# Where the compressed-value product and two spare transposes stand between the matmuls of a hybrid attention layer

## The chip, the cores and the metric

The kernel runs on one core of one Trainium2 chip. The metric is the device time of one execution in microseconds; the median of three runs of the kernel before is 369.53 us (369.27 to 370.02). A difference of about 0.2% (0.74 us) or less is not told apart from none.

## The reference

One decoder layer over 256 tokens of width 1024, in float32. What matters here:

```python
h = rmsnorm(x, norm1_g[layer])
proj = h @ w_in[layer]           # NSA q, 6 k/v parts, gates | MoBA q, k, v | 2 merge gates
...
y_nsa = nsa_attention(to_q(q), to_q(q_r), kc, vc, to_kv(k_s), to_kv(v_s),
                      to_kv(k_w), to_kv(v_w), gates)
...
y_moba = moba_attention(to_kv(qm), to_kv(km), to_kv(vm))
...
mixed = g_nsa * (y_nsa @ w_up_nsa[layer]) + g_moba * (y_moba @ w_up_moba[layer])
x = x + mixed @ w_out[layer]
h2 = rmsnorm(x, norm2_g[layer])
u = jax.nn.relu(h2 @ w_ff1[layer])
x = x + (u * u) @ w_ff2[layer]
```

Native sparse attention (NSA) adds three products per head: `gc[0] * o_cmp + gc[1] * o_sel + gc[2] * o_win`, over 15 compressed keys, the selected blocks and a window. With 256 tokens the selected blocks and the window are both all earlier tokens. MoBA is causal attention of 8 further heads.

## The kernel before, in words

Weights come in chunks of 1 MB (`CHUNKS`), one DMA each, three buffers deep. To multiply in float32, each chunk is split into a high part (`whi`, cast on ScalarE, L114) and a low part (`wlo`, difference on VectorE, L116) of type fp32r, and each product is three fp32r matmuls, a "triple" (`mm3`: high x high, high x low, low x high). All matmuls are recorded under one line, L243.

A chunk is a *slot*. `run_slot` issues the slot's matmuls in order and, at given fractions of it, the events that were registered with `at(position, function)`. The order on each engine is therefore written out by these positions; it doesn't depend on any planner. Chunks 0 to 11 are the projections (`xstat`: activations are the stationary operand, weights stream past, outputs 512 wide for q, qm, km and vm); chunk 11 (`C_VM + 1`) is the second half of vm. From chunk 12 on, the merge gates (gm, 12 to 19), then upn (20, 21), upm (22, 23), wout (24 to 27) and ff1 have the weights as stationary operand and stream 256 activations past (`wstat`). So chunk 11 ends with 128x512 matmuls, and chunk 12 begins with 128x256 ones. From chunk 31 on, ff2 and ff1 chunks alternate.

Attention runs in six *units* d = 0 to 5, threaded through the slots 9 to 21: units 0 to 3 are NSA (kind "n": one pair of heads p, the selected and the window branch, b = 1 and 2), units 4 and 5 are MoBA (kind "m": two pairs of heads). For unit d, slot 9 + 2d issues the scores (`d_scores`), the maxima on VectorE and the exponentials on ScalarE; slot 10 + 2d issues `d_norm` (VectorE, writes P at L580) and `d_trans`, near its end: twelve 128x128 transposes of P into the score banks Sa and Sb (L596), copied to PT by ScalarE (L598) and VectorE (L600). In the next slot, behind the next unit's scores, `d_pv` multiplies PT by the values: eight fp32 matmuls with 64 output rows each, two of them side by side in the array (128\*64). Here this is called the *P-V break*: the streams of full-array fp32r matmuls stop, and a few instructions of other shapes and types stand between. `d_yevac` then reads the sum y in bank yb (ScalarE L628, VectorE L629). Each fp32 matmul shows as two passes in the trace.

In an NSA unit, y has a further summand, the *compressed product*: one fp32 matmul of the block-diagonal compressed values (`bdv`) with the transposed compressed probabilities (`pcT`). In the kernel before it is the last thing that `d_trans` issues, and it opens the sum (start flag).

Behind unit 5's P-V break, in slot 21, the rest of upn, then upm, wout and the first ff1 chunk and a half are one unbroken run of 128x256 fp32r matmuls, until `x1_rows` transposes x in the middle of slot 29 (L883).

A helper from the ff2 stage, used in `seven_mms` for the last triple ahead of an ff1 chunk, issues a 512-wide triple as two 256-wide ones:

```python
def mm3_halves(o, lh, ll, rh, rl, first, last):
    r = mm3(o, lh, ll, rh, rl, first, last)[:int(first)]
    return r + [m for x in (slice(0, 256), slice(256, 512))
                for m in mm3(o[:, x], lh, ll, rh[:, x], rl[:, x], first, last)[int(first):]]
```

Of the kernel before, what the change touches and what calls it, by code (L numbers as in the profile page):

```python
# [36 lines left out]
C_KVB, C_Q, C_QM, C_KM, C_VM, C_GM, C_UPN, C_UPM, C_WOUT, C_FF = (  # L37
    2, 4, 6, 8, 10, 12, 20, 22, 24, 28)
# [7 lines left out]
def hybrid_layer(ctx: ExitStack, tc: tile.TileContext, gxd, w, w1c, small, const, gf, out):  # L46
    nc = tc.nc
    act, dve, pool, pe = nc.scalar, nc.vector, nc.gpsimd, nc.tensor
# [14 lines left out]
    def bank(tag, name):  # L63
        return ps.tile([128, 512], F32, name=name, tag=tag)
# [8 lines left out]
    def acc_tile():  # L73
        return next_bank("acc")
# [6 lines left out]
    def s_tile(x):  # L81
        if "s" not in pools:
            early_stack.close()
            pools["s"] = at_stack.enter_context(tc.tile_pool(name="ps_s", bufs=1, space=PS))
        return pools["s"].tile([128, 2, 512], F32, name="S" + "ab"[x])
# [35 lines left out]
    ident = cp.tile([128, 128], F32, name="ident")  # L121
# [120 lines left out]
    def mm(o, l, r, start, stop):  # L242
        pe.matmul(o, l, r, start=start, stop=stop, skip_group_check=True)  # L243

    def mm3(o, lh, ll, rh, rl, first, last):
        return [lambda: mm(o, lh, rh, first, False),
                lambda: mm(o, lh, rl, False, False),
                lambda: mm(o, ll, rh, False, last)]
# [7 lines left out]
    def xstat(c, n, accs, kts):  # L256

        r = []
        h, l = hi[c], lo[c]
        order = [(t, k) for t in range(2) for k in range(4)]  # L260
        if c < 2:
            order.sort(key=lambda e: e[1])
        for t, k in order:
            kt = kts[k]
            if True:
                lh, ll = (a[:, kt, t * 128:(t + 1) * 128] for a in (hTh, hTl))
                r += mm3(accs[t][:, :n], lh, ll, h[:, k * n:(k + 1) * n],
                         l[:, k * n:(k + 1) * n], kt == 0, kt == 7)
        return r

    def wstat(o, c, off, nk, ncol, ah, al, ks=None, first=0, last=None):
# [123 lines left out]
    bdv = ap_.tile([128, 4, 128], F32, name="bdv")  # L395
    pcT = ap_.tile([128, 256], F32, name="pcT")
# [5 lines left out]
    U = {}  # L402
# [120 lines left out]
    def s_views(d, t):  # L523
        S = U[d]["S"][1 - t]
        n = 128 + 128 * t
        return S[:, :, 0:2 * n].rearrange("p j (x k) -> p j x k", x=2)
# [56 lines left out]
    def d_trans(d):  # L583

        S, P = U[d]["S"], U[d]["P"]
        kind, p, _ = PAIRS[d][0]
        PT = ap_.tile([128, 4, 384], F32, name="PT")
        U[d]["PT"] = PT
        v = PT.rearrange("p (x j) k -> p j x k", x=2)
        for t, cs in ((1, (128, 256)), (0, (0,))):  # L590
            T = s_views(d, t)
            for j in range(2):
                for x in range(2):
                    for c in cs:
                        o = c % 256 if t == 0 else c - 128
                        pe.transpose(T[:, j, x, o:o + 128], P[:, 2 * x + j, c:c + 128], ident)  # L596
            if t:
                act.activation(v[:, :, :, 128:384], T, AF.Copy)  # L598
            else:
                dve.tensor_copy(v[:, :, :, 0:128], T)  # L600
        if d == 0:
            U["y"] = bank("yb", "yb").rearrange("p (a q) -> p a q", a=2)
        if kind == "n":
            mm(U["y"][:, p % 2], bdv[:, p, :], pcT, True, False)

    def d_pv(d):
        PT = U[d]["PT"]
        for x, (kind, p, b) in enumerate(PAIRS[d]):
            y = U["y"][:, p % 2]

            ts = (1, 0) if kind == "n" else (0, 1)
            for t in ts:
                n0 = 128 * t
                for j in range(2):
                    if kind == "n":
                        v = kvb[:, t, b * 128 + j * 64:b * 128 + (j + 1) * 64]
                    else:
                        v = vm[:, t, (2 * p + j) * 64:(2 * p + j + 1) * 64]
                    rhs = PT[:, 2 * x + j, 0:256] if t == 0 else PT[:, 2 * x + j, 256:384]
                    mm(y[j * 64:(j + 1) * 64, n0:256], v, rhs, kind == "m" and t == 0,  # L620
                       t == ts[1] and (kind == "m" or b == 2))

    def d_yevac(d):
        kind, p, _ = PAIRS[d][0]
# [6 lines left out]
    def unit_events(s):  # L631
        d = (s - 9) // 2
        if not 9 <= s <= 21:
            return
        if s % 2 == 0:
            at(0.1, d_norm, d)
            at(0.97 if s == 12 else 0.78, d_trans, d)
            return
        if d < 6:
            at(0.1, d_scores, d)  # L640
        if d > 0:
            at(0.1, d_pv, d - 1)
        if d < 6:
            at(0.11, d_max, d)
            at(0.2 if s > 12 else 0.5, d_exp, d, 1)
            at(0.22 if s > 12 else 0.52, d_exp, d, 0)
        if d > 0:
            at(0.12, d_yevac, d - 1)
# [4 lines left out]
    for sec, c0, n in groups:  # L653
        if sec in ("q", "qm", "km"):
            tm[sec] = ap_.tile([128, 2, 512], F32, name="qtm", bufs=2)
        if sec in ("kvb", "q"):
            accs = [ps_e.tile([128, 512], F32, name=f"{sec}acc{t}") for t in range(2)]
        else:
            accs = [acc_tile(), acc_tile()]
        for i in range(2):  # L660
            c = c0 + i
# [84 lines left out]
            elif i == 1:  # L746
                at(0.49 if sec == "vm" else 0.5, evac_tm, sec, 0, accs[0], n)
                if sec != "vm":
                    at(1.0, evac_tm, sec, 1, accs[1], n)
            run_slot(xstat(c, n, accs, range(4 * i, 4 * i + 4)))  # L750


# [30 lines left out]
    for g in range(8):  # L783
        c = C_GM + g
# [31 lines left out]
    for sec, c0, kind, evac in (("upn", C_UPN, "n", upn_evac), ("upm", C_UPM, "m", upm_evac)):  # L816
        for i in range(2):
            c = c0 + i
# [13 lines left out]
            accs = [acc_tile(), acc_tile()]  # L832
# [54 lines left out]
    for i in range(4):  # L887
        c = C_WOUT + i
# [144 lines left out]
    order = PARTS[0] + PARTS[1]  # L1033
# [226 lines left out]
```

## Time and profile before

| | |
|---|---|
| median of 3 runs | 369.53 us |
| profiled execution, its own time | 370.05 us |
| its span, first to last instruction | 368.2 us |
| TensorE busy, granted clock | 98%, 0.996 |
| VectorE, ScalarE busy | 87%, 66% |
| DMA | 66.34 MB, 180 GB/s |

In the rows quoted below, a timeline row has start, duration, engine, line, operation, output<-inputs, array rows\*columns, shape and count; neighbours of one name are merged into one row. Matmuls are pipelined: their durations overlap, and what counts is the distance between starts. A window row has the stretch, its width, and for each engine its busy time and the count of instructions, then the granted clock, the DMA share and GB/s. "Idle before" in brackets names what ended the engine's wait.

### The profile page before, as it was taken

The numbers are of one execution on the slowest core, as the hardware profiler recorded it, in microseconds if no ns is written. First come the engines' busy times: TensorE is split into PE (matmuls) and PEld (weight loads), VectorE is DVE, ScalarE is ACT, GpSimd is POOL, SyncE is SP. The second block draws the span as 40 slices with busy tenths as digits, with TensorE's granted clock in tenths as the row PEclk, the third lists the DMA queues.
The fourth block names the chain that finished last, engine by engine and source line by source line (L and its number), as shares of the span: only waits on it lengthen the run. The fifth ranks groups of instructions, "written<-read, shape, count | busy, mean of one in ns | idle before, by whom it ended". The sixth has DMA issues, their size and how long they took to land.

```text
span 368.2 us, 6524 instructions
## 1 busy us (share of the span) xinstructions
PE 360.7 (98%) x2658; PEld 331.8 (90%) x2658; DVE 320.6 (87%) x466; ACT 241.3 (66%) x367; POOL 3.4 (1%) x14
## 2 busy tenths in 40 slices
PE   8999999999999999999999999999999999999993
PEld 7997787879989999999999999999999999999983
DVE  4988979998967769767878999999999999999984
ACT  5984765777746657526455887867666777676623
POOL 1010000000000000000000000000000000000000
PEclk9999999999999999999999999999999999999998
DMA  7978326333433333533583666455556666554003
GB/s 275 407 306 309 128 105 228 114 116 122 182 136 134 115 117 129 215 116 114 189 326 121 227 228 216 171 180 178 188 212 230 228 230 226 195 189 180 12 3 114
DMA packets 11262, 66.34 MB, mean 180 GB/s; under 512 B 1248, under 2 KB 2784, under 8 KB 3936
## 3 DMA queue, kind: packets, MB, share of 16 engines
q1 hardware_dynamic: 10368, 64.35, 47.5%
q10 hardware_dynamic: 864, 1.57, 1.2%
q8 instruction: 21, 0.34, 0.4%
q14 instruction: 9, 0.07, 0.1%
HBM read 64.87 MB, written 1.05 MB: 179 GB/s over the span
## 4 chain that ended last, share of the span: by engine, by line
PE 96%; issue 1%; DVE 0%; POOL 0%; ACT 0%; POOLq 0%; DVEq 0%
PE acc L243 64%; PE o L243 10%; PE yb L243 5%; PE tp L243 4%; PE qacc L243 3%; PE kvbacc L243 3%; PE Sa L243 2%; PE Sa L596 1%; PE tp L338 1%; PE yb L156 1%; PE Sb L596 1%; PE Sb L243 1%; PE o L883 0%; PE tp L409 0%; DVE x L1137 0%
## 5 line engine op out<-in xcount | busy, mean ns | idle before, releaser
L116 DVE TENSOR_TENSOR wlo<-raw,whi 128x1024 fp32r<-128x1024 f32 (+3 forms) x83 | 105.0, 1286 | 4.4 <-ACT whi L114 4.3
L114 ACT ACTIVATE whi<-raw 128x1024 fp32r<-128x1024 f32 (+3 forms) x82 | 89.9, 1118 | 25.9 <-PE acc L243 16.2
L243 PE MATMUL acc<-h2h,whi 128*128 128x256 f32 x256 | 71.0, 277 | 0.0
L243 PE MATMUL acc<-h2l,whi 128*128 128x256 f32 x256 | 70.9, 277 | 0.0
L243 PE MATMUL acc<-h2h,wlo 128*128 128x256 f32 x256 | 70.8, 277 | 0.0
L243 PEld LDWEIGHTS acc<-h2l,whi 128*128 128x128 f32 x256 | 48.2, 188 | 0.0
L243 PEld LDWEIGHTS acc<-h2h,whi 128*128 128x128 f32 x256 | 48.1, 188 | 0.0
L243 PEld LDWEIGHTS acc<-h2h,wlo 128*128 128x128 f32 x256 | 48.1, 188 | 0.0
L986 ACT ACTIVATE whi<-wt 128x2048 fp32r<-128x2048 f32 x14 | 26.9, 1922 | 29.0 <-PE acc L243 28.1
L243 PE MATMUL acc<-hTh,wlo 128*128 128x256 f32 x128 | 36.8, 287 | 0.0
L243 PE MATMUL acc<-hTl,whi 128*128 128x256 f32 x128 | 35.7, 279 | 0.0
L243 PE MATMUL acc<-hTh,whi 128*128 128x256 f32 x128 | 35.7, 279 | 0.0
L988 DVE TENSOR_TENSOR wlo<-wt,whi 128x2048 fp32r<-128x2048 f32 x14 | 32.0, 2284 | 0.1
L243 PEld LDWEIGHTS acc<-hTh,wlo 128*128 128x128 f32 x128 | 24.3, 190 | 1.4 <-issue 1.3
L243 PE MATMUL acc<-whi,hTh 128*128 128x512 f32 (+1 forms) x64 | 25.3, 395 | 0.0
L243 PE MATMUL acc<-wlo,hTh 128*128 128x512 f32 (+1 forms) x64 | 25.0, 391 | 0.0
L243 PE MATMUL acc<-whi,hTl 128*128 128x512 f32 (+1 forms) x64 | 24.6, 385 | 0.0
L979 DVE TENSOR_TENSOR sl<-raw,sh 128x1536 fp32r<-128x1536 f32 x14 | 24.5, 1750 | 0.0
L243 PEld LDWEIGHTS acc<-hTh,whi 128*128 128x128 f32 x128 | 24.0, 188 | 0.1
L243 PEld LDWEIGHTS acc<-hTl,whi 128*128 128x128 f32 x128 | 24.0, 188 | 0.0
L977 ACT ACTIVATE sh<-raw 128x1536 fp32r<-128x1536 f32 x14 | 20.8, 1488 | 3.3 <-PE acc L243 3.3
L243 PE MATMUL acc<-mxh,whi 128*128 128x256 f32 x64 | 18.0, 281 | 0.0
(308 smaller groups left out, 868.4 us busy)
## 6 DMA issues: line engine op xcount, KB each, us to landing
raw<-in_ff_dram SPq DMA_DIRECT2D x32, 1024.0 KB, 4.9
raw<-in_gm_dram SPq DMA_DIRECT2D x8, 1024.0 KB, 4.8
raw<-in_wout_dram SPq DMA_DIRECT2D x4, 1024.0 KB, 4.8
raw<-in_q_dram SPq DMA_DIRECT2D x2, 1024.0 KB, 5.0
raw<-in_qm_dram SPq DMA_DIRECT2D x2, 1024.0 KB, 6.3
raw<-in_km_dram SPq DMA_DIRECT2D x2, 1024.0 KB, 6.2
raw<-in_vm_dram SPq DMA_DIRECT2D x2, 1024.0 KB, 4.8
raw<-in_upn_dram SPq DMA_DIRECT2D x2, 1024.0 KB, 5.9
```

The source lines that it names most:

```text
L114: act.activation(hi[c][:, a:b], raw[c][:, a:b], AF.Copy)
L116: dve.tensor_tensor(lo[c][:, a:b], raw[c][:, a:b], hi[c][:, a:b].bitcast(F32), op=ALU.subtract)
L156: pe.transpose(warm[:, 0:128], ident, ident)
L243: pe.matmul(o, l, r, start=start, stop=stop, skip_group_check=True)
L338: pe.transpose(tp[:, j * 256 + t * 128:j * 256 + t * 128 + 128], src[:, t, (2 * i + j) * 128:(2 * i + j + 1) * 128], ident)
L596: pe.transpose(T[:, j, x, o:o + 128], P[:, 2 * x + j, c:c + 128], ident)
L977: act.activation(singles[c][0], v, AF.Copy)
L979: dve.tensor_tensor(singles[c][1], v, singles[c][0].bitcast(F32), op=ALU.subtract)
L986: act.activation(hi[c], v, AF.Copy)
L988: dve.tensor_tensor(lo[c], v, hi[c].bitcast(F32), op=ALU.subtract)
```

## The change

Three edits, all on TensorE's instructions; the other engines' instructions and their order stay the same.

1. In units 0 to 3 the compressed product is issued at the end of `d_pv` instead of the end of `d_trans`. It now closes the sum, and the first P-V matmul opens it. For this the wide half (256 columns) comes ahead of the narrow half (128 columns) in NSA units, as it already did in MoBA units.
2. Behind unit 5's P-V matmuls two transposes of the identity are issued into the free score bank; nothing reads them.
3. The last triple of chunk 11 goes through `mm3_halves`: six 256-wide matmuls instead of three 512-wide ones.

```diff
@@ xstat @@
-                r += mm3(accs[t][:, :n], lh, ll, h[:, k * n:(k + 1) * n],
-                         l[:, k * n:(k + 1) * n], kt == 0, kt == 7)
+                f = mm3_halves if c == C_VM + 1 and (t, k) == order[-1] else mm3
+                r += f(accs[t][:, :n], lh, ll, h[:, k * n:(k + 1) * n],
+                       l[:, k * n:(k + 1) * n], kt == 0, kt == 7)
@@ d_trans @@
         if d == 0:
             U["y"] = bank("yb", "yb").rearrange("p (a q) -> p a q", a=2)
-        if kind == "n":
-            mm(U["y"][:, p % 2], bdv[:, p, :], pcT, True, False)
@@ d_pv @@
-            ts = (1, 0) if kind == "n" else (0, 1)
-            for t in ts:
-                n0 = 128 * t
+            for t, n0 in ((0, 0), (1, 128)):
                 for j in range(2):
...
-                    mm(y[j * 64:(j + 1) * 64, n0:256], v, rhs, kind == "m" and t == 0,
-                       t == ts[1] and (kind == "m" or b == 2))
+                    mm(y[j * 64:(j + 1) * 64, n0:256], v, rhs,
+                       t == 0 and (kind == "m" or b == 1), t == 1 and kind == "m")
+        if kind == "n":
+            mm(y, bdv[:, p, :], pcT, False, True)
+        elif d == 5:
+
+            pace = s_tile(0)
+            for x in range(2):
+                pe.transpose(pace[:, 0, x * 128:(x + 1) * 128], ident, ident)
```

Unit 1 on TensorE, behind its transposes (slot 12 ends, slot 13 begins with unit 2's scores). Before:

```order
L596 MATMUL Sa<-ident,P 128x128 x8
L596 MATMUL Sb<-ident,P 128x128 x4
L243 MATMUL yb<-pcT,bdv 128x256
L243 MATMUL acc<-hTh,wlo 128x256
L243 MATMUL acc<-hTh,whi 128x256
L243 MATMUL acc<-hTl,whi 128x256
L243 MATMUL acc<-hTh,wlo 128x256
L243 MATMUL acc<-hTh,whi 128x256
L243 MATMUL acc<-hTl,whi 128x256
L243 MATMUL Sa<-kswh,qrh 128x512 x2
```

and now:

```order
L597 MATMUL Sa<-ident,P 128x128 x8
L597 MATMUL Sb<-ident,P 128x128 x4
L243 MATMUL acc<-hTh,wlo 128x256
L243 MATMUL acc<-hTh,whi 128x256
L243 MATMUL acc<-hTl,whi 128x256
L243 MATMUL acc<-hTh,wlo 128x256
L243 MATMUL acc<-hTh,whi 128x256
L243 MATMUL acc<-hTl,whi 128x256
L243 MATMUL Sa<-kswh,qrh 128x512 x2
```

The product (yb<-pcT,bdv) has left this place; six gate matmuls follow the transposes directly, then the scores. Unit 1's P-V break, a little later in slot 13, before:

```order
L243 MATMUL Sb<-kswh,qrl 128x256 x2
L243 MATMUL yb<-PT,kvb 64x128 x2
L243 MATMUL yb<-PT,kvb 64x256 x2
L243 MATMUL yb<-PT,kvb 64x128 x2
L243 MATMUL yb<-PT,kvb 64x256 x2
L243 MATMUL acc<-hTh,wlo 128x256
L243 MATMUL acc<-hTh,whi 128x256
```

and now:

```order
L243 MATMUL Sb<-kswh,qrl 128x256 x2
L243 MATMUL yb<-PT,kvb 64x256 x2
L243 MATMUL yb<-PT,kvb 64x128 x2
L243 MATMUL yb<-PT,kvb 64x256 x2
L243 MATMUL yb<-PT,kvb 64x128 x2
L243 MATMUL yb<-pcT,bdv 128x256
L243 MATMUL acc<-hTh,wlo 128x256
L243 MATMUL acc<-hTh,whi 128x256
```

The halves have changed places, and the product stands between the P-V matmuls and the gate stream. Unit 5's P-V break in slot 21 (vm are MoBA's values, yThn and yTln the high and low parts of the NSA result that stream past the upn weights) was before:

```order
L243 MATMUL yb<-PT,vm 64x256 x2
L243 MATMUL yb<-PT,vm 64x128 x2
L243 MATMUL yb<-PT,vm 64x256 x2
L243 MATMUL yb<-PT,vm 64x128 x2
L243 MATMUL acc<-yThn,wlo 128x256
L243 MATMUL acc<-yThn,whi 128x256
```

and is now:

```order
L243 MATMUL yb<-PT,vm 64x256 x2
L243 MATMUL yb<-PT,vm 64x128 x2
L243 MATMUL yb<-PT,vm 64x256 x2
L243 MATMUL yb<-PT,vm 64x128 x2
L624 MATMUL Sa<-ident 128x128 x2
L243 MATMUL acc<-yThn,wlo 128x256
L243 MATMUL acc<-yThn,whi 128x256
```

The two transposes (Sa<-ident) are new; the rows around them are as before.

## The prediction

> **What bounds the kernel now.** I read the page first, then the waits of TensorE's weight loads, then the busy time by stretches, then the timeline at the places that the change touches.
>
> ```profile
> span 368.2 us, 6524 instructions
> PE 360.7 (98%) x2658; PEld 331.8 (90%) x2658; DVE 320.6 (87%) x466; ACT 241.3 (66%) x367; POOL 3.4 (1%) x14
> PE 96%; issue 1%; DVE 0%; POOL 0%; ACT 0%; POOLq 0%; DVEq 0%
> PEld acc L243 <- DVE wlo L116: 0.6, 2, 0.3
> PEld Sa L596 <- DVE P L580: 0.2, 1, 0.2
> ```
>
> The chain that ended last is TensorE for 96%, and from the first P-V break on it waits for another engine only once: the 0.2 us before unit 1's transposes (the 0.6 lies in the first 40 us). So the time is the sum of the distances between the starts of TensorE's instructions. Those distances are not the same everywhere. The windows below hold nothing but 128x256 fp32r matmuls of the same array shape:
>
> ```profile
> core 0: us, PE busy (x), PEclk, DMA share, GB/s
> 82.80:88.20 5.40, 5.40 (x48) 1.00 0.55 194
> 94.00:103.40 9.40, 9.40 (x81) 1.00 0.39 149
> 110.00:119.30 9.30, 9.30 (x81) 1.00 0.42 152
> 126.50:135.10 8.60, 8.60 (x78) 1.00 0.39 139
> 142.00:150.50 8.50, 8.50 (x78) 1.00 0.41 156
> 155.50:202.50 47.00, 47.00 (x402) 1.00 0.47 170
> 204.70:212.50 7.80, 7.80 (x71) 1.00 0.46 167
> ```
>
> A count takes in those already running at the window's edge, so I add one duration (0.28 us) to the width: 47.28/402 = 117.6 ns a matmul in the long window, but 8.08/71 = 113.8, 8.88/78 = 113.8 and 8.78/78 = 112.6 ns in the fast ones. The granted clock is 1.00 in all. A stream keeps the pace with which it starts: the long one is slow from end to end, across chunks, banks and weights. From the first and the last start I get it more exactly:
>
> ```profile
> 152.01 0.28 PE L243 MATMUL acc<-yThn,whi 128*128 128x256 f32 x1
> ...
> 152.46 0.28 PE L243 MATMUL acc<-yTln,whi 128*128 128x256 f32 x1
> ...
> 155.14 0.39 PE L243 MATMUL acc<-yThn,wlo 128*128 128x256 f32 x1
> 155.37 0.28 PE L243 MATMUL acc<-yThn,whi 128*128 128x256 f32 x1
> ...
> 202.59 0.28 PE L243 MATMUL acc<-h2h,wlo 128*128 128x256 f32 x1
> ...
> 204.02 0.60 PE L883 MATMUL o<-ident,gx 128*128 128x128 f32 x4
> 204.37 0.37 PE L243 MATMUL acc<-h2h,whi 128*128 128x256 f32 x1
> 204.58 0.28 PE L243 MATMUL acc<-h2l,whi 128*128 128x256 f32 x1
> ...
> 212.52 0.28 PE L243 MATMUL acc<-h2h,wlo 128*128 128x256 f32 x1
> ```
>
> Between 155.37 and 202.59 lie 401 steps: 47.22/401 = 117.8 ns. Between 204.58 and 212.52 lie 70: 7.94/70 = 113.4 ns. The difference, **4.3 ns a matmul**, is the prize. The stream at 155.14 begins straight behind a P-V break (unit 5's), the one at 204.37 behind transposes. Of the five streams that begin straight behind a P-V break, three are slow (94, 110, 155) and two fast (126, 142). The one behind transposes at 204.37 is fast, and so is the short one behind unit 5's twelve transposes: four steps from 152.01 to 152.46 are 112 ns each.
>
> **The change, part by part.**
>
> *The compressed product moves to the end of the break.* In the row order before, it stands behind unit 1's transposes:
>
> ```profile
> 88.50 1.09 PE L596 MATMUL Sa<-ident,P 128*128 128x128 f32 x8
> 89.43 0.60 PE L596 MATMUL Sb<-ident,P 128*128 128x128 f32 x4
> 89.86 0.60 PE L243 MATMUL yb<-pcT,bdv 128*128 128x256 f32 x2
> 90.42 0.28 PE L243 MATMUL acc<-hTh,whi 128*128 128x256 f32 x1
> 90.54 0.28 PE L243 MATMUL acc<-hTl,whi 128*128 128x256 f32 x1
> 91.09 0.50 PE L243 MATMUL Sa<-kswh,qrh 64*128 64x512 f32 x2
> ...
> 93.78 0.38 PE L243 MATMUL acc<-hTh,wlo 128*128 128x256 f32 x1
> 94.00 0.28 PE L243 MATMUL acc<-hTh,whi 128*128 128x256 f32 x1
> ```
>
> Its two passes run from 89.86 to 0.12 before 90.42, that is 0.44 us, and nothing of it is hidden. It costs 0.44 at the new place too, so the move itself is worth 0. Behind the break, the first acc matmul takes 0.22 to the next (93.78 to 94.00) where a step is 0.12: its weight load lies open for 0.10. Now the product's load lies open there and acc's load is covered by a 0.22 pass. If the product's load is as long as acc's, that is an even exchange; if it is as short as a P-V load, up to 0.06 is gained in each of units 1 to 3. I take 0. In unit 0 a transpose stood behind the break, whose load is shorter, so some 0.05 is lost there; that ends in the wait at 88.50 (below).
>
> Behind the two passes comes the acc stream. The rows at 90.42 and 90.54 show such a beginning, before only of five or a dozen matmuls. I count it as fast, since nothing lies open there. Units 1 and 2 then gain 79 steps (the windows' 81 without the two already running) of 4.3 ns each: **2 x 0.34 = 0.68 us**. Unit 3's stream (126) is fast already: 0.
>
> With the product gone from behind the transposes, TensorE would reach the next scores 0.44 earlier, at 90.65. Their tile Sa has first to be copied by ScalarE, whose copy ends at 89.69 + 1.02 = 90.71:
>
> ```profile
> 89.69 1.02 ACT L598 ACTIVATE PT<-Sa 128x1024 f32<-128x1024 f32 x1 [2.03 <-PE Sa L596]
> 86.62 1.83 DVE L580 TENSOR_TENSOR P<-P,ust 128x512 f32<-128x512 f32 x2
> ```
>
> So a new wait of 0.06 and a semaphore's way arises in unit 1; behind the scores stand unit 1's P-V and the whole stream. I count **+0.10** (bounds 0 and 0.3). In units 2 and 3 some ten more acc matmuls (1.1 us) lie between the transposes and the scores, so nothing waits. ScalarE's evacuation of y, now 0.44 later behind the break, holds up only the exponentials, which wait for VectorE's maxima anyway.
>
> *The P-V order, wide half first.* Unit 0 has the narrow half first, unit 4 the wide one:
>
> ```profile
> 76.02 1.52 PE L243 MATMUL yb<-PT,kvb 128*64 128x128 f32 x16
> 77.47 0.66 PE L338 MATMUL tp<-ident,qtm 128*128 128x128 f32 x4
> ...
> 139.81 1.52 PE L243 MATMUL yb<-PT,vm 128*64 128x256 f32 x16
> 141.26 0.38 PE L243 MATMUL acc<-hTh,wlo 128*128 128x256 f32 x1
> ```
>
> Both take 1.45 us to the next instruction, so the order is worth 0.
>
> *Two idle transposes behind unit 5's break.* A transpose is 0.108 (89.43 to 89.86 is four), two are 0.22. The first one's load lies open instead of acc's 0.10: 88.50 to 89.43 is eight transposes and 0.06 more. Cost 0.22 + 0.06 - 0.10 = **+0.18**. They wait for nothing: the tile's last readers made the PT that the break has just read. The gain is the stream behind them, 401 steps of 4.3 ns: **-1.74 us**.
>
> *The triple in two parts.* Three 128x512 become six 128x256, at most 0.03 longer. What follows are 47 slow matmuls up to 88.3 (the window from 82.80 has 5.68/48 = 118 ns), worth 0.20 at the fast pace. But unit 1's transposes wait for VectorE's P, which ends at 86.62 + 1.83 = 88.45 and hangs on the exponentials, not on this stream. TensorE only waits longer there. Value **0** (at most -0.2 if P comes earlier).
>
> [...]
>
> *Who must follow.* Arriving earlier helps only if the data does too.
>
> ```profile
> 194.43 0.42 DVE L863 TENSOR_TENSOR gx<-gx,acc 128x256 f32<-128x256 f32 x1 [1.34 <-PE acc L243]
> 210.70 1.08 DVE L938 TENSOR_TENSOR al<-aq,ah 128x896 fp32r<-128x896 f32 x1
> 213.09 0.39 PE L243 MATMUL o<-sh,al 128*128 128x512 f32 x1
> ...
> 197.00:343.00 146.00, 146.00 (x1046) 136.66 (x1046) 145.36 (x159) 107.48 (x97) 0.00 (x0) 1.00 0.55 202
> ```
>
> From 197 on VectorE (third figure, 145.36 of 146.00) is as full as TensorE, which is the danger. But until 194.43 it waits for TensorE, so it starts that stage earlier by what is gained until then. Only the steps from 194.4 to 202.6, about 70 x 4.3 = 0.30 us, eat into its lead. The lead is smallest at al: done at 211.78, and its load begins one step ahead of 213.09, at 212.86, so 1.08 us. It shrinks to 0.78. No wait.
>
> Sum: +0.10 + 0.18 - 0.68 - 1.74 = **-2.14 us**. The profiled execution took 370.05 us with a span of 368.2, so it lies 0.5 above the median of 369.53; I take the sum off the median: **367.4 us**.
>
> **The rivals.**
>
> *Unit 5 stays slow* (9%). Two transposes are fewer than the twelve and sixteen that stand ahead of the fast streams of the rows, and the pace may need more. Against it: from the second one on, each load lies under a stream as it does there. The 1.74 falls away: 369.1.
>
> *The product does not set the pace* (8%). Two fp32 passes behind a change of array shape are nowhere in the trace; units 1 and 2 keep 117.8: 368.1.
>
> *No pace is carried* (5%): what makes a stream slow is tied to its place and not to what stands ahead, and only the added work is left, 0.10 + 0.18: 369.8. [...]
>
> *VectorE does not follow* (5%). If its stage hangs on something that I didn't see, TensorE can gain no more than its lead of 1.08: 368.5.
>
> *Slower: the pace goes by the phase at which a stream begins* (5%). Streams 126 and 142 are fast behind the same kind of break as the slow 94 and 110, which speaks for a phase; the same pattern in two neighbouring units speaks for the instructions around it. If the shift turned those two slow (2 x 79 x 4.3 = +0.68) and won no other, with 0.28 of added work it would be 370.5. It decides from the point where the lost streams outweigh the won ones.
>
> **How the numbers follow.** The forecast has 68%, its own range 366.9 to 367.9 (the wait 0 to 0.3, the loads up to -0.18, the triple up to -0.2, pace 4.0 to 4.6 ns). Together with 368.1 and 368.5 that is 81%, so the range is 366.8 to 368.6. About 0.2%, 0.74 us, is what a measurement can tell: faster (below 368.8) has 81%, within it (369.1 and 369.8) 14%, slower 5%.
>
> **What would show it.** The window from unit 5's break to the x1 transposes should hold its 403 matmuls in about 45.7 us instead of 47.5, durations of 276 ns instead of 281; streams 94 and 110 the same. The wait before unit 1's transposes should grow to about 0.35 us. A wait of PE for ACT PT should appear near 90.7. The forecast is wrong if the long stream keeps 118 ns, or if PE waits for DVE behind 205.

## The result, and the profile after

The changed kernel takes 368.14 us (median of six runs, 367.58 to 368.51) beside 369.69 us (six runs, 369.27 to 370.09) for the kernel before on the same chip: a ratio of 0.9948, interval 0.9934 to 0.9962. That is 1.55 us less; 2.14 us had been predicted. The profiled execution took 368.34 us.

The page of the changed kernel, span, TensorE and the chain of waits by engine:

```profile
span 366.6 us, 6535 instructions
PE 358.8 (98%) x2663; PEld 330.3 (90%) x2663; DVE 320.1 (87%) x466; ACT 241.4 (66%) x367; POOL 3.4 (1%) x14
PE 94%; issue 2%; ACT 1%; DVE 1%; POOL 0%; POOLq 0%; DVEq 0%
```

The span falls by 1.6 us (from 368.2), and TensorE's busy time by 1.9 (from 360.7), though five more matmuls run. ScalarE and VectorE now show on the chain with 1% each. The windows of the changed kernel, in the streams behind the breaks of units 1, 2, 4 and 5, and in the ff2 stage:

```profile
core 0: us, PE busy (x) PEld busy (x) DVE busy (x) ACT busy (x) POOL busy (x), PEclk, DMA share, GB/s
94.30:103.60 9.30, 9.30 (x81) 9.30 (x81) 7.29 (x14) 6.21 (x20) 0.00 (x0) 1.00 0.40 143
110.30:119.20 8.90, 8.90 (x81) 8.90 (x80) 6.78 (x14) 6.18 (x20) 0.00 (x0) 1.00 0.44 157
...
141.60:150.40 8.80, 8.80 (x80) 8.80 (x79) 8.21 (x14) 6.19 (x20) 0.00 (x0) 1.00 0.46 164
155.60:200.90 45.30, 45.30 (x402) 45.30 (x401) 35.03 (x49) 22.64 (x30) 0.00 (x0) 1.00 0.47 173
195.40:341.40 146.00, 146.00 (x1048) 136.65 (x1048) 145.56 (x159) 107.96 (x97) 0.00 (x0) 1.00 0.54 202
```

With one duration (0.28 us) added to each width, unit 5's stream runs at 45.58/402 = 113.4 ns a matmul, where it had 117.6; unit 2's at 9.18/81 = 113.3, where it had been slow. But unit 1's stream is still slow: 9.58/81 = 118.3 ns. VectorE stays full behind it (145.56 of 146).

The beginning of unit 5's stream and its end, TensorE's timeline of the changed kernel:

```profile
153.68 1.52 PE L243 MATMUL yb<-PT,vm 128*64 128x256 f32 x16
155.13 0.44 PE L624 MATMUL Sa<-ident 128*128 128x128 f32 x2
155.32 0.36 PE L243 MATMUL acc<-yThn,wlo 128*128 128x256 f32 x1
155.52 0.28 PE L243 MATMUL acc<-yThn,whi 128*128 128x256 f32 x1
155.64 0.28 PE L243 MATMUL acc<-yTln,whi 128*128 128x256 f32 x1
155.76 0.28 PE L243 MATMUL acc<-yThn,wlo 128*128 128x256 f32 x1
155.88 0.28 PE L243 MATMUL acc<-yThn,whi 128*128 128x256 f32 x1
156.00 0.28 PE L243 MATMUL acc<-yTln,whi 128*128 128x256 f32 x1
156.11 0.28 PE L243 MATMUL acc<-yThn,wlo 128*128 128x256 f32 x1
...
201.11 1.91 PE L886 MATMUL o<-ident,gx 128*128 128x128 f32 x16
```

From 155.52 to 201.11 are 402 steps in 45.59 us; before they took 47.34 (155.37 to 0.12 behind 202.59). That is 1.75 us less. The rows also show something that the prediction did not look for: the first four steps are still of 0.12 us (117, 118, 122 and 118 ns by the records), and only then does the stream fall into 113 ns.

Around unit 1's transposes, the changed kernel's timeline (rows of VectorE, TensorE's loads and ScalarE):

```profile
86.75 1.83 DVE L581 TENSOR_TENSOR P<-P,ust 128x512 f32<-128x512 f32 x2
...
88.63 0.85 PEld L597 LDWEIGHTS Sa<-ident,P 128*128 128x128 f32 x8 [0.40 <-DVE P L581]
...
89.82 1.03 ACT L599 ACTIVATE PT<-Sa 128x1024 f32<-128x1024 f32 x1 [2.03 <-PE Sa L597]
...
90.90 0.19 PEld L243 LDWEIGHTS Sa<-kswh,qrh 64*128 64x128 f32 x2 [0.24 <-ACT PT L599]
```

TensorE waits 0.40 for P instead of 0.2, and then newly 0.24 for ScalarE's copy of Sa. From the transposes to the scores it takes 2.27 us (88.63 to 90.90) instead of 2.59 (88.50 to 91.09): 0.32 less, where the product that left had taken 0.44. So the new wait costs 0.12.

A last place, al in the ff2 stage of the changed kernel:

```profile
209.40 1.08 DVE L941 TENSOR_TENSOR al<-aq,ah 128x896 fp32r<-128x896 f32 x1
...
211.27 0.40 PE L243 MATMUL o<-sl,ah 128*128 128x512 f32 x1
211.50 0.39 PE L243 MATMUL o<-sh,al 128*128 128x512 f32 x1
```

al is done at 210.48, and its load begins at the matmul before, 211.27: a lead of 0.79.

### The profile page after: what moved, and what is told of

Its sections match the earlier page's. It is cut to its first block, busy times and chain, and to the rows that moved or that the text cites. A ratio compares the mean times of both kernels' runs of the same rounds, so it can differ in the third digit from the quotient of the medians.

```text
span 366.6 us, 6535 instructions
## 1 busy us (share of the span) xinstructions
PE 358.8 (98%) x2663; PEld 330.3 (90%) x2663; DVE 320.1 (87%) x466; ACT 241.4 (66%) x367; POOL 3.4 (1%) x14
## 4 chain that ended last, share of the span: by engine, by line
PE 94%; issue 2%; ACT 1%; DVE 1%; POOL 0%; POOLq 0%; DVEq 0%
PE acc L243 61%; PE o L243 10%; PE yb L243 6%; PE tp L243 4%; PE qacc L243 3%; PE kvbacc L243 3%; PE Sa L243 2%; PE Sa L597 1%; PE tp L339 1%; ACT P L567 1%; PE yb L156 1%; PE Sb L597 1%; PE Sb L243 1%; PE o L886 0%; DVE P L581 0%
## 5 line engine op out<-in xcount | busy, mean ns | idle before, releaser
L243 PE MATMUL acc<-whi,hTh 128*128 128x512 f32 (+2 forms) x65 | 25.6, 394 | 0.1
L243 PE MATMUL acc<-wlo,hTh 128*128 128x512 f32 (+2 forms) x65 | 25.1, 386 | 0.0
L243 PE MATMUL acc<-whi,hTl 128*128 128x512 f32 (+2 forms) x65 | 24.8, 382 | 0.0
```

## The experiments

Executions differ by up to 1 us in when they reach the first attention unit (70.07 to 71.12 us in these traces), and nearly all of that is there at the first q matmul already (24.22 to 25.26 us). So I compare distances inside an execution: from unit 1's first transpose to unit 2's, from unit 2's to unit 3's, and from unit 5's to the x1 transposes (by TensorE's records). A count in a window of 9 us that begins 0.5 us into unit 1's or unit 2's stream, or of 45 us in unit 5's, tells the pace: 78 or 79 and 384 or 385 is slow, 82 and 399 is fast. In the expectations the prediction's own theory (what stands ahead of a stream sets its pace; A) is set against others, above all that the exact moment of its beginning does (B).

| kernel | unit 1 to 2, us | unit 2 to 3 | unit 5 to x1 | count unit 1 | unit 2 | unit 5 |
|---|---|---|---|---|---|---|
| before | 14.93 | 15.89 | 52.14 | 79 | 78 | 385 |
| changed | 15.03 | 15.61 | 50.56 | 79 | 82 | 399 |
| transposes alone | 14.95 | 15.89 | 50.56 | 79 | 79 | 399 |
| product alone | 14.71 | 15.56 | 52.13 | 82 | 82 | 384 |
| triple alone | 14.93 | 15.95 | 52.15 | 79 | 78 | 385 |
| without transposes | 15.06 | 15.55 | 52.14 | 79 | 82 | 385 |
| without the two-part triple | 15.05 | 15.55 | 50.55 | 79 | 82 | 399 |
| one transpose | 15.05 | 15.94 | 52.22 | 79 | 79 | 384 |
| one matmul, 256 columns | 15.05 | 15.55 | 52.26 | 79 | 82 | 385 |
| two transposes ahead of the break | 14.70 | 15.90 | 52.38 | 82 | 79 | 385 |
| three transposes | 14.69 | 15.57 | 50.64 | 82 | 82 | 399 |
| four transposes | 14.70 | 15.90 | 50.77 | 82 | 79 | 399 |
| one matmul, 64 columns | 14.70 | 15.90 | 52.26 | 82 | 79 | 384 |
| transposes in unit 1 too | 15.27 | 15.61 | 50.57 | 78 | 82 | 399 |

**One part at a time.** First the two transposes alone, added to the kernel before:

```diff
@@ d_pv, end @@
+        if d == 5:
+
+            pace = s_tile(0)
+            for x in range(2):
+                pe.transpose(pace[:, 0, x * 128:(x + 1) * 128], ident, ident)
```

> Of the three edits, only the two idle transposes behind unit 5's P-V break. Theory (what stands ahead sets the pace): the 403 matmuls behind them run at 113.4 ns a step, so that stretch takes about 45.8 us instead of 47.5, and for 0.2 us of added work the kernel takes 1.55 us less than before, about as much as the whole change. Streams behind units 1 and 2 stay at 118 ns, those behind units 3 and 4 at 113. Rival (the phase at which a stream begins sets the pace): the stream behind unit 5 may fall either way, and the neighbours too; if it stays slow, the kernel takes 0.2 us more than before.

368.19 us, ratio 0.9962 (0.9947 to 0.9977). Unit 5 to x1 falls by 1.58 us, as in the whole change, and nothing else moves. The transposes carry nearly all of the gain. Then the product alone (the P-V halves' new order and start flags go with it, as in the whole change; they are left out here, at the dots):

```diff
@@ d_trans @@
-        if kind == "n":
-            mm(U["y"][:, p % 2], bdv[:, p, :], pcT, True, False)
@@ d_pv @@
...
+        if kind == "n":
+            mm(y, bdv[:, p, :], pcT, False, True)
```

> Only the move of the compressed product (with the P-V halves' new order), without the transposes and without the triple in two parts. Theory: behind units 1 and 2 the product now stands ahead of the stream; unit 2's stream is at 113 ns as with the whole change. Unit 1's stream was slow with the whole change; if that came from the two-part triple ahead of it, it is fast here (another 0.34 us gained). Unit 5's stream is slow. Time 0 to 0.4 us below before. Rival (phase): units 1 and 2 fall as chance has it.

Its profiled execution has both streams fast (the first two windows), and unit 5's slow:

```profile
93.92:102.92 9.00, 9.00 (x82) 1.00 0.37 134
109.48:118.48 9.00, 9.00 (x82) 1.00 0.42 153
154.69:199.69 45.00, 45.00 (x384) 1.00 0.44 160
```

Unit 1 to 2 is 0.22 shorter (predicted +0.10 - 0.34 = -0.24) and unit 2 to 3 0.33 (predicted 0.34). Yet over ten timed runs it is 369.74 us, ratio 0.9991 (0.9979 to 1.0004): the some 0.5 us of the profiled execution is not in the median, so by the times the move alone is worth nothing that can be measured. The triple alone:

```diff
-                r += mm3(accs[t][:, :n], lh, ll, h[:, k * n:(k + 1) * n],
...
+                f = mm3_halves if c == C_VM + 1 and (t, k) == order[-1] else mm3
+                r += f(accs[t][:, :n], lh, ll, h[:, k * n:(k + 1) * n],
...
```

> Only the last triple of chunk 11 in two parts. Theory: the gate matmuls behind it run at 113 ns instead of 118, TensorE reaches unit 1's transposes 0.2 us earlier and waits there 0.2 us longer for VectorE's P (0.4 us instead of 0.2). Time as before within 0.1 us. If P came earlier too, up to 0.2 us would be gained.

370.02 us, ratio 1.0005 (0.9994 to 1.0016): nothing. Its effect is real but covered. Ahead of unit 1's transposes TensorE now waits longer:

```profile
PEld Sa L597 <- DVE P L581: 0.4, 1, 0.4
```

**One part left out.** Without the transposes (the four added lines deleted from the changed kernel):

> The whole change without the two idle transposes. Theory: the stream behind unit 5 goes back to 118 ns a step (47.5 us), and the kernel is 1.5 us slower than with them, within 0.3 us of the kernel before: what the product's move gains behind unit 2 (0.34 us) is lost by the later P of unit 1 (0.1 us) and the wait for ScalarE's copy (0.2 us). Rival (phase): the stream may be fast without them, then the kernel is at 367.9 to 368.0 us.

369.07 us, ratio 0.9982 (0.9973 to 0.9992), and unit 5 to x1 is back at 52.14. What the other two parts give is 0.7 us or less; that is more than the 0.3 that had been expected at most, and the profiled execution, at 369.96 us, is the slowest of its ten. Without the two-part triple (the third diff above reversed):

> The whole change without the triple in two parts. In the runs so far unit 1's stream was fast with the product moved alone (93.4 on, 113.3 ns) and slow with the product and the two-part triple together (117.8 ns, twice). Theory A (the two-part triple shifts what comes before unit 1's break and so costs unit 1 its pace): all streams behind the breaks are fast here, the distance from unit 1's transposes to unit 2's is 14.7 us instead of 15.0, and the kernel is 0.3 us faster than the whole change and 2.1 us faster than before. Theory B (unit 1's pace is chance): it may be slow here too, and the kernel takes as long as the whole change within 0.1 us.

367.74 us, ratio 0.994 (0.9927 to 0.9953). That can't be told from the changed kernel's 0.9948; the triple in two parts isn't needed. Unit 1's stream is slow here too, where A had expected it fast, so the triple does not decide it.

**What decides unit 5's stream.** One transpose instead of two:

```diff
-            for x in range(2):
+            for x in range(1):
```

> The whole change with one idle transpose behind unit 5's break instead of two. Theory (it is enough that the stream's first weight load lies under an instruction of another kind): the stream is fast with one too, and from unit 5's transposes to x1's it takes 50.45 us, 0.11 less than with two. Rival (phase): 0.11 us less of added work shifts the start; the stream may be slow, then 52.0 us.

370.4 us over ten runs (369.23 to 370.98), ratio 1.0004 (0.9993 to 1.0015). The gain is gone, and A missed: it had held one covered load to be enough. From here on A means two or more. In its timeline the stream begins at the same 0.12 us a step and stays there:

```profile
155.79 0.33 PE L624 MATMUL Sa<-ident 128*128 128x128 f32 x1
155.87 0.36 PE L243 MATMUL acc<-yThn,wlo 128*128 128x256 f32 x1
156.07 0.28 PE L243 MATMUL acc<-yThn,whi 128*128 128x256 f32 x1
156.19 0.28 PE L243 MATMUL acc<-yTln,whi 128*128 128x256 f32 x1
156.31 0.28 PE L243 MATMUL acc<-yThn,wlo 128*128 128x256 f32 x1
```

The same instruction kind as the stream's instead of transposes, one 256-wide matmul into the idle tile:

```diff
-            for x in range(2):
-                pe.transpose(pace[:, 0, x * 128:(x + 1) * 128], ident, ident)
+            mm(pace[:, 0, 0:256], hi[C_UPN + 1][:, 0:128], yTh["n"][:, 0, :], True, True)
```

> The whole change with one idle 128x256 fp32r matmul of the stream's own kind (its result goes to the free score bank) behind unit 5's break instead of the two transposes. Theory (another kind of instruction must stand ahead): the stream only begins one step earlier with an open load, stays slow at 118 ns, 52.25 us from unit 5's transposes to x1's. Rival (phase): may be fast, 50.5 us.

Slow: 52.26, which is 52.14 and the one step more (a single run, 369.9 us). The two transposes ahead of unit 5's P-V matmuls instead of behind:

```diff
@@ d_pv, first line @@
+        if d == 5:
+            pace = s_tile(0)
+            for x in range(2):
+                pe.transpose(pace[:, 0, x * 128:(x + 1) * 128], ident, ident)
@@ d_pv, end @@
-        elif d == 5:
-            pace = s_tile(0)
-            for x in range(2):
-                pe.transpose(pace[:, 0, x * 128:(x + 1) * 128], ident, ident)
```

> The whole change with the two idle transposes ahead of unit 5's P-V matmuls instead of behind them, so that the stream again begins straight behind the break, only some 0.2 us later. Theory: what stands directly ahead counts; the stream is slow at 118 ns, 52.3 us from unit 5's transposes to x1's. Rival (what stands ahead of the break, or the moment at which it begins, sets the pace; units 3 and 4 are fast straight behind their breaks): fast, 50.6 us.

Slow in unit 5, at a cost of 0.24 us for nothing (52.38; a single run, 369.5 us): ahead of the break the transposes did not help. But its other windows are the surprise:

```profile
93.80:102.80 9.00, 9.00 (x82) 1.00 0.38 139
109.36:118.36 9.00, 9.00 (x79) 1.00 0.43 156
155.19:200.19 45.00, 45.00 (x385) 1.00 0.43 161
```

Unit 1 is fast and unit 2 slow, the other way round than in the changed kernel, though the two programs are the same up to unit 5. The kernel with one transpose, again the same up to there, has both slow:

```profile
94.73:103.73 9.00, 9.00 (x79) 1.00 0.39 143
110.67:119.67 9.00, 9.00 (x79) 1.00 0.38 149
156.37:201.37 45.00, 45.00 (x384) 1.00 0.46 160
```

So the instructions ahead do not settle the pace behind the product; something outside of the program up to there does. That called for more counts and kinds behind unit 5's break (`range(3)`, `range(4)`, and a single fp32r matmul of 64 columns), and for the same two transposes at another place. First three and four transposes:

> The change, with three idle transposes behind unit 5's break instead of two. Theory A, as now read (two or more covered loads make the stream fast, one does not): the stream of 403 is fast, and the x1 transposes start 50.56 + 0.11 = 50.67 us after unit 5's first transpose. Theory B (a stream falls into one of two lasting rhythms by the exact moment, to some ns, at which it begins): a third transpose moves that moment by 0.108 us, and either rhythm can come; the slow one would give 52.42 us (52.22 as measured behind one transpose, and two more of 0.108).

> The change, with four idle transposes. Theory A: fast, 50.56 + 0.22 = 50.78 us from unit 5's first transpose to the x1 transposes. Theory B: fast or slow (52.53 us). If two, three and four are all fast and one is slow, A stands for this place; if three or four is slow, it falls.

Both are fast, the window of 45 us with three and then, of the other kernel, with four:

```profile
155.92:200.92 45.00, 45.00 (x399) 1.00 0.49 174
```

```profile
156.13:201.13 45.00, 45.00 (x399) 1.00 0.47 174
```

The distances, 50.64 and 50.77, are the forecast 50.67 and 50.78 within 0.03 (single runs, 368.42 and 368.63 us). Then 64 columns:

```diff
-            for x in range(2):
-                pe.transpose(pace[:, 0, x * 128:(x + 1) * 128], ident, ident)
+            mm(pace[:, 0, 0:64], hi[C_UPN + 1][:, 0:128], yTh["n"][:, 0, 0:64], True, True)
```

> The change, with a single fp32r matmul of 64 columns in the idle tile instead of the two transposes: no other kind of instruction and one load that lies open, as it did in the kernel with a 256-wide one there, which was slow. Theory A: slow, 52.14 to 52.25 us from unit 5's first transpose to the x1 transposes. Theory B: the beginning is moved by some 0.03 to 0.1 us and the stream may turn fast, 50.4 to 50.6 us; a fast stream here would show that neither transposes nor covered loads are needed.

```profile
155.76:200.76 45.00, 45.00 (x384) 1.00 0.43 160
```

Slow (a single run, 370.04 us). At this place, then, A as read since the miss with one transpose was right each time: at least two transposes straight ahead of the stream, and it is fast. Last, the kernel without the two-part triple and with two transposes behind unit 1's product as well:

```diff
-        elif d == 5:
-
-            pace = s_tile(0)
+        if d in (1, 5):
+            pace = s_tile(0)[:, 0] if d == 5 else bank(turn["acc"][0], "acc")
             for x in range(2):
-                pe.transpose(pace[:, 0, x * 128:(x + 1) * 128], ident, ident)
+                pe.transpose(pace[:, x * 128:(x + 1) * 128], ident, ident)
```

> The change without the triple in two parts, and with two idle transposes also behind unit 1's compressed product, into the acc bank that comes next. Theory A: unit 1's stream of 79 steps becomes fast (it was slow without them): from unit 1's first transpose to unit 2's 15.05 + 0.22 - 0.35 = 14.92 us. Theory B: slow or fast; slow is 15.27 us. In both the stream behind unit 5 stays fast, with 50.56 us to the x1 transposes, unless what changes in unit 1 moves its beginning.

```profile
95.14:104.14 9.00, 9.00 (x78) 1.00 0.33 126
110.99:119.99 9.00, 9.00 (x82) 1.00 0.41 150
156.43:201.43 45.00, 45.00 (x399) 1.00 0.49 174
```

A falls here: two transposes straight ahead, and unit 1's stream is slow; the distance is the 15.27 us of the slow case (a single run, 368.95 us). The two places differ in more than the unit, though: in unit 1 the transposes stand behind the fp32 product and write the acc bank that comes next, in unit 5 they stand behind P-V matmuls and write the free score bank. The same is seen elsewhere: behind the sixteen x1 transposes the stream is fast in 12 of the 14 profiled kernels, but slow in the kernels with one transpose and with the 256-wide matmul. There it costs 0.3 us more up to the end. In the kernel with one transpose, and then in the changed one, 7 us of that stream:

```profile
205.60:212.60 7.00, 7.00 (x62) 1.00 0.46 159
```

```profile
203.30:210.30 7.00, 7.00 (x64) 1.00 0.51 180
```

## Why the prediction was right and where it was wrong

**The total.** 368.14 us lies in the range of 366.8 to 368.6, but outside the forecast's own 366.9 to 367.9 and beside the 368.1 of the rival "the product does not set the pace". As a difference it is 1.55, beside that rival's 1.46 (2.14 less 0.68). So the total alone does not bear out the forecast, and where it fell within the range owes something to luck, since the paces of units 1 and 2 differ between executions (below). The parts have to be taken one by one.

**Unit 5's two transposes: right in size, and shown to be what does it; not shown is why.** -1.74 + 0.18 = -1.56 was predicted; the distance from unit 5 to x1 shows -1.58, with the transposes alone as well as in the whole. Without them nothing is gained (52.14). The rivals "unit 5 stays slow" and "no pace is carried" fall. Identical matmuls at a granted clock of 1.00 ran at 113.3 ns in one kernel and at 117.8 in the next. The prediction's "A stream keeps the pace with which it starts" does not hold as it stands, since this stream began with four steps of 117 to 122 ns and was fast after them; what a stream keeps is the pace that it has settled on.

The Trainium skill's page "TensorE: Matmul & The Clock Gate", section "Back-to-back issue gap", gives for an isolated matmul one warm gap, the free size over 2.4 GHz and 2.5 ns, and says that a stream of weight loads and matmuls is spaced by both. By that formula 256 columns would take an estimated 109 ns; both paces measured here lie above it, and the section names no second pace.

**Unit 1's stream: the step that failed.** The prediction said of the stream behind the product: "I count it as fast, since nothing lies open there. Units 1 and 2 then gain". The evidence was a beginning of five or six matmuls in the trace before, too short to see where a stream settles. In the changed kernel's trace unit 2 gained 0.28 us and unit 1 nothing: its stream kept 118 ns, and only the wait was left (+0.10 from unit 1 to unit 2, where -0.24 was predicted). That accounts for 0.34 of what is missing. Another 0.07 is the short stream of 15 matmuls at 104.89, slow in the changed kernel and fast before (15 x 4.4 ns), which is why unit 2 shows 0.28 and not 0.34. Some 0.15 lies ahead of unit 1's transposes: 0.08 from the first q matmul to unit 0's transposes, where the programs are the same and the 14 traces scatter over 0.09 us, and 0.07 from there to unit 1's (see unit 0 below). -2.14 + 0.34 + 0.07 + 0.15 = -1.58, which is what the two traces show from the first q matmul to the end.

Over all kernels the term of 0.34 a stream is right in size but not certain: with the product straight ahead, unit 1 was fast in 5 of 10 profiled executions and unit 2 in 7 of 11. Eight of these kernels are the same program up to unit 5, and of them unit 1 was fast in 4 and unit 2 in 4, in all four combinations. With the product at its old place both were slow in 3 of 3. So moving the product gives each of these two streams roughly an even chance of its 0.34, on what was seen. The rival "the product does not set the pace" priced both as lost; one half of it came true. The rival by phase comes nearest for these two streams: what decides isn't in the program up to there. That it is the moment of the beginning was not shown, and the rival's price was wrong, since it had all of the gains lost.

**The new wait: right.** +0.10 was counted; the scores came 0.12 later than without it. The wait itself reads 0.24, but that is idle time of the load queue, which runs one step (0.11) ahead of the matmuls.

**Unit 0's loss: a smaller step that failed.** The prediction let unit 0's 0.05 end in the wait ahead of unit 1's transposes. It does not end there. From unit 0's first transpose to unit 1's it takes 17.85 or 17.86 us in the three kernels with the product at its old place, and 17.90 to 17.92 in the eleven with it moved. P itself comes later, since ScalarE's exponentials for it follow its evacuation of vm, and that waits for TensorE. Before, and then in the changed kernel:

```profile
80.25 0.69 ACT L314 ACTIVATE vm<-acc,rstd 128x512 f32<-128x512 f32 x1 [1.48 <-PE acc L243]
80.83 0.47 ACT L566 ACTIVATE P<-Sa,ust 128x256 f32<-128x256 f32 x1
```

```profile
80.36 0.69 ACT L315 ACTIVATE vm<-acc,rstd 128x512 f32<-128x512 f32 x1 [1.48 <-PE acc L243]
80.95 0.47 ACT L567 ACTIVATE P<-Sa,ust 128x256 f32<-128x256 f32 x1
```

Counted from unit 0's first transpose (70.64 and 70.71), the exponentials begin at 10.19 and now at 10.24. So the wait for P was no slack for what delays TensorE further ahead; ScalarE's new share of the chain that ended last lies here.

**The triple in two parts: right.** 0 was predicted, 1.0005 measured, with TensorE's wait for P at 0.40 (0.35 was named). It does turn its stream fast, to 113.3 ns in all nine kernels that have it, where the five without have 117.8; but P sets that point.

**P-V order and the product's own cost: right within 0.05.** From unit 3 to 4, where the pace is fast in both kernels, it is 15.84 before and 15.86 now.

**VectorE follows: right.** al's lead went from 1.08 to 0.79 us; 0.78 had been worked out. From x1 to the end it is 165.45 us before and 165.44 now.

**Left open.** I did not find what fixes the pace. Two, three and four transposes behind unit 5's break gave fast streams in 6 of 6 kernels, and none, one, or one fp32r matmul slow ones in 8 of 8, with one profiled execution each; but two transposes failed behind unit 1's product. Whether the loads, the moment at which the stream begins, or both together decide isn't told apart by these runs, since each added instruction also moves that moment.

## What to carry to other kernels

Where an engine never waits and the time still differs, divide the width of a stream by its count: a long stream of equal matmuls can be 4% off its other pace with busy time, clock and waits all looking perfect. A couple of idle instructions ahead of the longest such stream may be worth trying, but it must be measured, in the place itself: the recipe held behind one break and failed behind another. Read how a stream settles from its first dozen steps, not from its first five, and believe a gain of one trace only when identical code shows it in another execution too.

## What the hardware showed that was not expected

A stream of 128x256 fp32r matmuls has two lasting paces, 113.33 and 117.78 ns by the records of its 390 later steps, and nothing in between. It finds one of them within its first twelve steps (for example 117, 118, 122, 118, 114, 113 to the fast one, or 118, 117, 118, 118 and so on), and then no stream of 40 or more, in any of the 14 profiled kernels, left it ahead of the x1 transposes, through changes of bank, of weights and of chunk.

The pace isn't set by the program alone: eight kernels, one profiled execution each and identical up to unit 5, show all four combinations of slow and fast in units 1 and 2. By the distances in the table that is worth up to 0.7 us, while the changed kernel's six times spread over 0.9 (367.58 to 368.51).

Elsewhere the place alone told the pace. The streams behind units 3 and 4 were fast in all 14 profiled kernels, in unit 3 with the product ahead as well as without it, and so were the thirteen ff1 streams of 48 matmuls each behind x1.
